# Head sums filled to the whole array, an offset joined to the bonus, and sums of squares in groups of four, in a kernel of an RWKV block, two expert layers and two attention blocks

## The chip, the cores and the metric

The kernel runs as one program on one core of a Trainium2 chip. The metric is the device time of one execution in microseconds (us), from a median of several runs. The core's engines are TensorE (PE; PEld is its loading of stationary operands), VectorE (DVE), ScalarE (ACT), GpSimd (POOL) and SyncE (SP, which here issues most DMA transfers). Each takes its own list of instructions in order, and the lists are held together by semaphores.

## What is computed

All arrays are float32; x has 512 rows of width 1024, a context has 256 rows. The program has two parts, one behind the other. The first has two layers of a token mixer and an expert layer of 16 experts: the mixer of layer 0 is a Fourier transform, that of layer 1 an RWKV recurrence in two directions. The second has two layers of four kinds of attention and an MLP. What the change touches of it:

```python
def rwkv_output(y, r, v, g, k_dirs, r_k, lnx_w, lnx_b, wo, dtype):
    mu = jnp.mean(y, axis=-1, keepdims=True)               # y: 512 x 16 heads x 64
    var = jnp.mean(jnp.square(y - mu), axis=-1, keepdims=True)
    yn = (y - mu) * lax.rsqrt(var + LNX_EPS)
    yn = yn.reshape(bsz, t, D_MODEL) * lnx_w + lnx_b
    bonus = sum(jnp.sum(r * k_d * rk, axis=-1, keepdims=True) for k_d in k_dirs) * v
    out = (yn + bonus.reshape(bsz, t, D_MODEL)) * g
    return out @ wo

def rms_norm(x, g):                                        # many of these
    return x * lax.rsqrt(jnp.mean(x * x, axis=-1, keepdims=True) + EPS) * g

h2 = rms_norm(x, norm2[l])                                 # second part, layer l
x = x + jnp.square(jax.nn.relu(h2 @ w_up[l])) @ w_down[l]
```

## The kernel before, in words

Activations lie transposed: the 1024 features are 8 blocks of 128 partitions (ND = 8), the tokens run along the free axis. A large product is written as three products of halves (`mm3`, lines L930 to L932): each operand is split by `split` (L894 on ACT, L895 on DVE or POOL) into a high and a low part, here `whi` and `wlo` for the weights that `wload` brings, block by block, through a DMA on SP into `wraw` (L914).

**The order.** The program is written down in Python with generators that take turns; a scheduler then orders each engine's list by its own estimates. Tiles come from pools with a fixed number of buffers, so a write into a buffer waits until its last reader is done.

**Sums of squares.** A norm over the 1024 features of a token needs a sum over partitions. Class `Sums` does it: `add` squares one block of features into a tile `sq` (L956 on POOL or DVE, L958 on ACT) and calls `flush`, which multiplies a block of ones (128 rows, 32 columns) by `sq` into the PSUM tile `nps` (L967). Block dt goes to the group of columns dt mod 4 of the array, so that four groups of 32 columns collect two blocks each. `flush` issues one product for each `sq` as soon as more than `lag` are outstanding. `col` copies the four groups (L976), adds them up (L979), and `rsqrt_col` and `bcast_col` take the root and spread it over partitions (L986 to L999). These sums stand in the norm ahead of the recurrence, in that ahead of the second expert layer (whose router products `lgT`, L801, also use a quarter of the columns each; its `psh`, L812, use the whole array), in the norm ahead of the MLP (`n2`, added to while `wo` is computed, with the products `up_` behind it) and in the norm of the next layer (added to while the MLP's second product `dn` is computed, one block of features after the other; each is 24 or more products of 128x512). How many `sq` may be outstanding follows from the number of buffers of the tag that `e.sq` names.

**The key projection** (`k_ahead`, `k_evac`, eight blocks m of 128 features). For block m, PE makes `cps` (running sums of the decay, L1275), ACT makes `Pe` and `Pi` of it (exponentials, L1276 and L1277, which need a table load on ACT), the projection `pj` gives `kt`, its norm per head goes over `kn`, `rn` (L1294 on ACT, L1295 on DVE) and `rnb` to `kk` (L1305). DVE and POOL make `kd`, `bkt` and `art` of them, which DMAs store. Last come `bon`, the head sums for the bonus (L1338, PE), `vm`, bonus times value (L1339, DVE), and the DMA that stores `vm` as `sp_bv` (L1340). The recurrence then loads `bk` and `ar` back (L1406, L1407; first used by `bkp`, L1439).

**The output of the recurrence** (`c_out`). Four token tiles of 128; `chain(t)` makes for each: `mu`, head means (L1671), `od`, the difference (L1672), its square `osq` on ACT (L1673), `var`, head sums of the squares with the table `hsum` as stationary operand (128 rows, 16 columns; eight products, L1677), `ors`, root and reciprocal on 16 partitions (L1679, L1680), `rsb`, the way back from 16 heads to 128 features with `hback` as stationary operand (16 rows, 128 columns, L1687), `gps`, the gate (128 rows, 128 columns, L1688). DVE multiplies `od` by weight and `rsb` (L1691), adds offset and bonus (L1692) and multiplies by the gate (L1694); ACT and DVE or POOL split the result into `oh` and `ol`. `project` multiplies by `rw_wo` (`wo`, 128x256 products) and adds to x (L1710). `weave` lets chains 1 and 2 go first, then chains 0 and 3 beside the products for tiles 1 and 2, then the products for tiles 0 and 3.

```python
hback = pa.tile([16, ND, P], F32, name="hback")
nc.sync.dma_start(hback, e.d["k_hback"].rearrange("p (a b) -> p a b", a=ND))
...
weave((chain(1), 12.0), (chain(2), 12.0))
weave((chain(0), 12.0), (chain(3), 12.0), (project(slice(1, 3)), 18.0))
weave((project(slice(0, 4, 3)), 1.0))
```

Of the kernel before, what the change touches and what calls it, by code (L numbers as in the profile page):

```python
# [11 lines left out]
F32 = mybir.dt.float32  # L12
F32R = mybir.dt.float32r
I32 = mybir.dt.int32
AF = mybir.ActivationFunctionType
ALU = mybir.AluOpType
# [3 lines left out]
P = 128  # L20
D = 1024
ND = 8
T = 512
# [16 lines left out]
def host_tables():  # L40
# [67 lines left out]
    a = np.zeros((P, 16))  # L108
# [14 lines left out]
    sel = np.zeros((P, ND, 16))  # L123
    for dt in range(ND):
        sel[:64, dt, 2 * dt] = 1.0
        sel[64:, dt, 2 * dt + 1] = 1.0
    add("hsum", sel.reshape(P, 128))
# [651 lines left out]
def route(e, l, pr, pq, pp, rt, NTt, hD, V, posm, before, after):  # L779
# [71 lines left out]
    e.sq = dict(tag="sq", bufs=4)  # L851
# [90 lines left out]
class Sums:  # L942


    def __init__(self, e, pool, pp, n, ndt=ND, tag="mm"):
        self.e, self.pool, self.pp, self.n, self.ndt, self.tag = e, pool, pp, n, ndt, tag
        self.ng = min(4, ndt)
        self.ps = pp.tile([P, 512], F32, name="nps0", tag=tag)
        self.due = []
# [12 lines left out]
    def flush(self, lag):  # L962
        e = self.e
        while len(self.due) > lag:
            dt, sq = self.due.pop(0)
            j = 32 * (dt % self.ng)
            e.nc.tensor.matmul(self.ps[j:j + 32, :self.n], e.t("ones")[:, 0:32], sq, start=dt < self.ng,  # L967
                               stop=dt + self.ng >= self.ndt, tile_position=(0, j))
# [117 lines left out]
def c_proj(e, sp, tg, PL, ch, h):  # L1086
    nc, tc = e.nc, e.tc
    tt_ = nc.vector.tensor_tensor
    with ExitStack() as ctx:
# [190 lines left out]
        def k_evac(m, pss):  # L1280
# [58 lines left out]
            tt_(vm, flat(ps, 4), vm, ALU.mult)  # L1339
            nc.sync.dma_start(sp["bv"][:, m, :], vm)  # L1340
# [289 lines left out]
def c_out(e, sp, tg, Y):  # L1630
# [4 lines left out]
    with ExitStack() as ctx:  # L1635
# [9 lines left out]
        hback = pa.tile([16, ND, P], F32, name="hback")  # L1645
        nc.sync.dma_start(hback, e.d["k_hback"].rearrange("p (a b) -> p a b", a=ND))
# [13 lines left out]
        hsum = e.tc_("hsum").rearrange("p (a b) -> p a b", a=ND)  # L1660
        nc.sync.dma_start(e.x, sp["x"])

        def chain(t):
# [12 lines left out]
            for dt in range(ND):  # L1676
                nc.tensor.matmul(ps[:16, :P], hsum[:, dt, :], sq[:, dt, :], start=dt == 0, stop=dt == 7)  # L1677
            rs = pw.tile([16, P], F32, name="ors")
            nc.scalar.activation(rs, ps[:16, :P], AF.Sqrt, bias=eps[:16], scale=1.0 / 64)  # L1679
            nc.vector.reciprocal(rs, rs)  # L1680
            yield 3.0
            for hf in range(2):
                ps = pm.tile([P, 4, P], F32, name="rsb", tag="mm")
                pg = pm.tile([P, 4, P], F32, name="gps", tag="mm")
                for b in range(4):
                    dt = hf * 4 + b
                    nc.tensor.matmul(ps[:, b, :], hback[:, dt, :], rs, start=True, stop=True)  # L1687
                    nc.tensor.matmul(pg[:, b, :], g2[:, dt * P:(dt + 1) * P], tg[:, ts], start=True, stop=True)  # L1688
                for b in range(4):
                    dt = hf * 4 + b  # L1690
                    nc.vector.scalar_tensor_tensor(d_[:, dt, :], d_[:, dt, :], e.pv["rw_lnx_w"][:, dt:dt + 1], ps[:, b, :], op0=ALU.mult, op1=ALU.mult)  # L1691
                    nc.vector.scalar_tensor_tensor(d_[:, dt, :], d_[:, dt, :], e.pv["rw_lnx_b"][:, dt:dt + 1], bv[:, dt, ts], op0=ALU.add, op1=ALU.add)  # L1692
                hs = slice(hf * 4, hf * 4 + 4)
                tt_(d_[:, hs, :], pg, d_[:, hs, :], ALU.mult)  # L1694
                split(e, d_[:, hs, :], oh[:, hs, ts], ol[:, hs, ts], nc.gpsimd if hf else nc.vector)
                yield 3.0
# [161 lines left out]
def stage_e(e, l, n1, more):  # L1858
# [4 lines left out]
    with ExitStack() as c1:  # L1863
# [6 lines left out]
        e.sq = dict(tag="u", bufs=3)  # L1870
# [3 lines left out]
        for fq in range(4):  # L1874
            up = (pw.tile([P, ND, T], F32R, name="uph"), pw.tile([P, ND, T], F32R, name="upl"))
            for f in range(8):
# [4 lines left out]
                u = pw.tile([P, T], F32, name="u", tag="u", bufs=3)  # L1881
# [25 lines left out]
def attention(e, l, c2, mixT, n1, pq, rsb2, w_up):  # L1907
# [316 lines left out]
    for _ in out_proj((4, 5), lambda m: n2.add(m, e.x[:, m, :], nc.gpsimd if m % 2 else None, lag=2)):  # L2224
        pass
# [124 lines left out]
```

## Time and profile before

| | |
|---|---|
| median of 3 runs | 3890.82 us (3889.8 to 3914.53) |
| profiled execution | 3894.26 us, of which the span is 3892.5 |
| mean granted clock of TensorE | 0.93 |
| busy: PE, DVE, ACT, POOL | 92%, 45%, 29%, 14% |
| sums of squares (L967) | 156 records, median 592 ns |
| key projection, from its first to its last block | about 1100 to 1285 us |
| output of the recurrence | about 1744 to 1839 us |
| MLP of the two attention layers, product dn | around 3084 to 3140 and 3836 to 3880 us |

All durations are of the one profiled execution. A float32 product that isn't split into halves by the program stands as two records in the trace, so the number of records is twice that of the products for `nps`, `var`, `rsb` and `gps`. A record's length covers the time until its last column has left the array; what a product costs in a stream is the distance from its start to the next start. The granted clock is a share of 2.4 GHz: 0.5 is the lower level, 1.2 GHz, and a window's number is the mean over both. Busy time of a group counts overlapping records once, its mean doesn't.

### The profile page before, as it was taken

To read this page: it belongs to the slowest core of one execution; us is meant where nothing else is said; L and a number is where in the kernel's file an instruction comes from. 1 tells how busy PE (TensorE), PEld (TensorE's weight loads), DVE (VectorE), ACT (ScalarE), POOL (GpSimd) and SP (SyncE) were. 2 spreads that over 40 slices of the span, in tenths; PEclk is the share of its full clock that TensorE was granted. 3 is DMA by queue.
4 is the path that set the end of the run, shared out by engine and by line. 5 is a ranking of instruction groups with operands and counts; after the bars stand their busy time and mean duration, and the time that the engine had idled before them with its cause. 6 is when DMAs were issued, how large, how long until landed. Compare 5 with 4: busy or idle time off the path is not lost. (4 is left out here: it accounts for less than half of the span.)

```text
span 3892.5 us, 66006 instructions
## 1 busy us (share of the span) xinstructions
PE 3585.0 (92%) x28088; PEld 2259.5 (58%) x28088; DVE 1762.6 (45%) x3424; ACT 1115.3 (29%) x1974; POOL 545.2 (14%) x429
## 2 busy tenths in 40 slices
PE   8889999978998686779999999999999989999999
PEld 4633333335777575668533324566788756567886
DVE  4512322246355566565221215865544458454443
ACT  3311111125366243332200002433322234342222
POOL 3100000002023122120100002220111222201111
PEclk8989999989998577788899999999999989999999
DMA  7489989934656644332899995111233321113332
GB/s 281 179 337 367 360 325 372 346 109 132 199 123 169 142 128 121 100 92 86 340 409 394 409 394 164 28 48 31 85 97 93 90 70 33 40 32 103 93 97 76
DMA packets 585853, 690.39 MB, mean 177 GB/s; under 512 B 178825, under 2 KB 454111, under 8 KB 585046
## 3 DMA queue, kind: packets, MB, share of 16 engines
q1 hardware_dynamic: 579344, 666.54, 50.6%
q10 hardware_dynamic: 3686, 11.09, 0.8%
q0 software_dynamic: 2528, 8.53, 0.6%
q8 instruction: 221, 3.62, 0.4%
q14 instruction: 74, 0.61, 0.0%
HBM read 646.24 MB, written 39.85 MB: 176 GB/s over the span
## 5 line engine op out<-in xcount | busy, mean ns | idle before, releaser
L894 ACT CAST whi<-wraw 128x1024 fp32r<-128x1024 f32 (+3 forms) x236 | 233.2, 989 | 707.2 <-issue 223.9
L641 PE MATMUL GU<-we,Xe 128*32 128x512 f32 x2048 | 304.4, 599 | 3.4 <-DVE hid L646 3.4
L895 DVE TENSOR_TENSOR wlo<-wraw,whi 128x1024 fp32r<-128x1024 f32 (+3 forms) x196 | 231.8, 1183 | 108.1 <-ACT whi L894 99.4
L666 PE MATMUL Y<-we,hidT 128*32 128x512 f32 x2048 | 261.3, 595 | 5.0 <-DVE Zc L698 3.5
L641 PE MATMUL GU<-we,Xq 128*32 128x512 f32 x2048 | 252.0, 611 | 0.0
L646 DVE TENSOR_TENSOR hid<-hid,GU 64x1536 f32<-64x1536 f32 (+1 forms) x32 | 47.7, 1491 | 359.4 <-ACT hid L645 359.4
L641 PE MATMUL GU<-we,Xc 128*32 128x512 f32 x1024 | 188.9, 596 | 0.0
L645 ACT ACTIVATE hid<-GU 64x1536 f32<-64x1536 f32 (+1 forms) x32 | 39.3, 1229 | 457.7 <-PE GU L641 457.7
L1884 POOL TENSOR_TENSOR u<-u 128x512 f32<-128x512 f32 x64 | 93.9, 1469 | 533.2 <-ACT uph L1883 533.2
L641 PEld LDWEIGHTS GU<-we,Xe 128*32 128x32 f32 x2048 | 78.8, 110 | 150.9 <-issue 145.2
L641 PEld LDWEIGHTS GU<-we,Xq 128*32 128x32 f32 x2048 | 67.7, 113 | 160.8 <-issue 157.9
L930 PE MATMUL pj<-hTh,whi 128*128 128x512 f32 (+1 forms) x352 | 154.5, 440 | 4.1 <-ACT hTh L1013 2.8
L666 PEld LDWEIGHTS Y<-we,hidT 128*32 128x32 f32 x2048 | 70.2, 110 | 148.1 <-issue 143.4
L932 PE MATMUL pj<-hTh,wlo 128*128 128x512 f32 (+1 forms) x352 | 148.7, 423 | 0.0
L931 PE MATMUL pj<-hTl,whi 128*128 128x512 f32 (+1 forms) x352 | 147.6, 419 | 0.0
L895 POOL TENSOR_TENSOR wlo<-wraw,whi 128x1024 fp32r<-128x1024 f32 x40 | 96.1, 2403 | 311.3 <-ACT whi L894 291.5
L930 PE MATMUL pj<-xh,whi 128*128 128x512 f32 (+1 forms) x320 | 118.2, 369 | 9.2 <-ACT whi L894 9.2
L1430 PE MATMUL Aps<-ar,bk 64*128 64x128 f32 (+1 forms) x768 | 98.3, 367 | 27.1 <-DVE GA L1434 25.1
L655 DVE COPY hidT<-htp 128x512 f32<-128x512 f32 (+1 forms) x48 | 27.6, 600 | 209.3 <-PE htp L654 121.4
L711 DVE SCALAR_TENSOR_TENSOR xres<-sps,mod,xres 128x512 f32<-128x512 f32 x128 | 89.0, 745 | 65.1 <-PE sps L710 64.5
L932 PE MATMUL pj<-xh,wlo 128*128 128x512 f32 (+1 forms) x320 | 115.4, 361 | 1.6 <-DVE wlo L895 1.6
L931 PE MATMUL pj<-xl,whi 128*128 128x512 f32 (+1 forms) x320 | 114.8, 359 | 0.0
(2151 smaller groups left out, 7929.4 us busy)
## 6 DMA issues: line engine op xcount, KB each, us to landing
we<-in_moe_wd_dram SPq DMA_DIRECT2D x128, 1024.0 KB
we<-in_moe_wg_dram SPq DMA_DIRECT2D x126, 1024.0 KB
we<-in_moe_wu_dram SPq DMA_DIRECT2D x126, 1024.0 KB
ada<-in_ada_w_dram SPq DMA_DIRECT2D x32, 1024.0 KB
wraw<-in_w_up_dram SPq DMA_DIRECT2D x64, 512.0 KB
wraw<-in_w_down_dram SPq DMA_DIRECT2D x64, 512.0 KB
wraw<-in_w_in_dram SPq DMA_DIRECT2D x42, 512.0 KB
adw<-in_ada_w_dram SPq DMA_DIRECT2D x32, 512.0 KB
```

The lines of the kernel that those rows point to most:

```text
L641: nc.tensor.matmul(GU[j:j + 32, g, :], xs[g][:, kk, :], ws[m][:, k, h * 512:(h + 1) * 512], start=kk == 0, stop=kk == 7, tile_position=(0, j))
L645: nc.scalar.activation(hid[up], GU[lo], AF.Silu)
L646: nc.vector.tensor_tensor(hid[up], hid[up], GU[up], ALU.mult)
L666: nc.tensor.matmul(Y[j:j + 32, 0, :], hidT[:, g, k, 32 * kh:32 * kh + 32], w[:, kh, h * 512:(h + 1) * 512], start=kh + k == 0, stop=kh * k ...
L711: nc.vector.scalar_tensor_tensor(r_[:, c, :], ps, g2[:, c, s:s + 1], r_[:, c, :], op0=ALU.mult, op1=ALU.add)
L894: e.nc.scalar.copy(hi, src)
L895: (eng or e.nc.vector).tensor_tensor(lo, src, hi, ALU.subtract)
L930: nc.tensor.matmul(ps, a[0], b[0], start=start, stop=False)
L931: nc.tensor.matmul(ps, a[0], b[1], start=False, stop=False)
L932: nc.tensor.matmul(ps, a[1], b[0], start=False, stop=stop)
L1430: nc.tensor.matmul(pss[hh][:, b, :64 * na], flat(4 * g + b)[hv[hh]], ar[hv[hh], 4 * g + b, 0:na, :], start=True, stop=True, tile_position= ...
L1884: nc.gpsimd.tensor_tensor(u, u, u, ALU.mult)
```

## The change

Three edits:

1. `flush` issues its products in steps: 4 where the tag of `sq` has more than four buffers, 2 where it has four, else 1, as soon as `lag` plus one step of them are outstanding. The tags get more buffers: six for `sq` behind the first expert layer's entry, and six for `u`, which the norm in the MLP uses. The norm ahead of the MLP has four buffers and its lag goes from 2 to 1.
2. In the key projection a new ACT operation adds the offset `rw_lnx_b` to `vm`, between DVE's product (L1339) and the DMA that stores it.
3. In `c_out`, `hback` becomes 128 rows with zeros in 112 of them (a memset on POOL ahead of the load), `hsum` is no longer a loaded table but is made on POOL (memset, then a copy) with 128 columns for each block, `ors` takes 128 partitions, and the 32 DVE operations that added offset and bonus become 8 that add the bonus alone, 512 columns each.

```diff
@@ class Sums
+        self.step = self.ng if e.sq["bufs"] > self.ng else min(2, self.ng) if e.sq["bufs"] > 3 else 1
@@ flush
-        while len(self.due) > lag:
-            dt, sq = self.due.pop(0)
-            j = 32 * (dt % self.ng)
-            e.nc.tensor.matmul(self.ps[j:j + 32, :self.n], e.t("ones")[:, 0:32], sq, start=dt < self.ng,
-                               stop=dt + self.ng >= self.ndt, tile_position=(0, j))
+        while len(self.due) >= lag + self.step:
+            for _ in range(self.step):
+                dt, sq = self.due.pop(0)
+                j = 32 * (dt % self.ng)
+                e.nc.tensor.matmul(self.ps[j:j + 32, :self.n], e.t("ones")[:, 0:32], sq, start=dt < self.ng,
+                                   stop=dt + self.ng >= self.ndt, tile_position=(0, j))
@@ buffers and lag
-    e.sq = dict(tag="sq", bufs=4)
+    e.sq = dict(tag="sq", bufs=6)
...
-        e.sq = dict(tag="u", bufs=3)
+        e.sq = dict(tag="u", bufs=6)
...
-                u = pw.tile([P, T], F32, name="u", tag="u", bufs=3)
+                u = pw.tile([P, T], F32, name="u", tag="u", bufs=6)
...
-    for _ in out_proj((4, 5), lambda m: n2.add(m, e.x[:, m, :], nc.gpsimd if m % 2 else None, lag=2)):
+    for _ in out_proj((4, 5), lambda m: n2.add(m, e.x[:, m, :], nc.gpsimd if m % 2 else None, lag=1)):
@@ k_evac
             tt_(vm, flat(ps, 4), vm, ALU.mult)
+            nc.scalar.activation(vm, vm, AF.Identity, bias=e.pv["rw_lnx_b"][:, m:m + 1])
             nc.sync.dma_start(sp["bv"][:, m, :], vm)
@@ c_out
-        hback = pa.tile([16, ND, P], F32, name="hback")
-        nc.sync.dma_start(hback, e.d["k_hback"].rearrange("p (a b) -> p a b", a=ND))
+        hback = pa.tile([P, ND, P], F32, name="hback")
+        nc.gpsimd.memset(hback, 0.0)
+        nc.sync.dma_start(hback[:16], e.d["k_hback"].rearrange("p (a b) -> p a b", a=ND))
+        hsum = pa.tile([P, ND * (P + 2)], F32, name="hsum")
+        nc.gpsimd.memset(hsum, 0.0)
+        nc.gpsimd.tensor_copy(hsum.rearrange("p (a b) -> p a b", a=ND)[:, :, 0:2], e.tc_("hsel").unsqueeze(1).to_broadcast([P, ND, 2]))
...
-        hsum = e.tc_("hsum").rearrange("p (a b) -> p a b", a=ND)
...
-                nc.tensor.matmul(ps[:16, :P], hsum[:, dt, :], sq[:, dt, :], start=dt == 0, stop=dt == 7)
-            rs = pw.tile([16, P], F32, name="ors")
-            nc.scalar.activation(rs, ps[:16, :P], AF.Sqrt, bias=eps[:16], scale=1.0 / 64)
+                nc.tensor.matmul(ps[:, :P], hsum[:, dt * P:(dt + 1) * P], sq[:, dt, :], start=dt == 0, stop=dt == 7)
+            rs = pw.tile([P, P], F32, name="ors")
+            nc.scalar.activation(rs, ps[:, :P], AF.Sqrt, bias=eps, scale=1.0 / 64)
...
-                    nc.vector.scalar_tensor_tensor(d_[:, dt, :], d_[:, dt, :], e.pv["rw_lnx_b"][:, dt:dt + 1], bv[:, dt, ts], op0=ALU.add, op1=ALU.add)
                 hs = slice(hf * 4, hf * 4 + 4)
+                tt_(d_[:, hs, :], d_[:, hs, :], bv[:, hs, ts], ALU.add)
```

How the lists of instructions change, at three places; a row is the line, the operation, what it writes and reads, its shape, and how many in a row. Lines of the changed kernel are up to five lower or three higher than before.

PE, in the product dn of layer 0's MLP (`dn` with two buffers' numbers, `uph` and `upl` its moving operand, `nps` the sum product, reading `sq` and the table of ones). Before, behind the first block of features:

```order
L931 MATMUL dn__24161<-upl,whi 128x512
L932 MATMUL dn__24161<-uph,wlo 128x512
L967 MATMUL nps_24118<-sq,tab 32x512
L930 MATMUL dn__24198<-uph,whi 128x512
L931 MATMUL dn__24198<-upl,whi 128x512
```

In the changed kernel, behind the fourth:

```order
L926 MATMUL dn__24257<-upl,whi 128x512
L927 MATMUL dn__24257<-uph,wlo 128x512
L965 MATMUL nps_24106<-sq,tab 32x512 x4
L925 MATMUL dn__24297<-uph,whi 128x512
L926 MATMUL dn__24297<-upl,whi 128x512
```

The sum products, one behind each of seven blocks and one at the end before, now stand in one row of four there and one at the end.

PE, in `c_out`, where the first two chains come to the head sums. Before:

```order
L1588 MATMUL Yps<-rc,SV 64x64 x16
L1677 MATMUL var<-osq,k_tabc 16x128 x16
L1687 MATMUL rsb<-ors,hback 128x128
L1688 MATMUL gps<-tg,g_15293 128x128
L1687 MATMUL rsb<-ors,hback 128x128
L1688 MATMUL gps<-tg,g_15293 128x128
```

In the changed kernel:

```order
L1587 MATMUL Yps<-rc,SV 64x64 x16
L1680 MATMUL var<-osq,hsum 128x128 x16
L1690 MATMUL rsb<-ors,hback 128x128
L1691 MATMUL gps<-tg,g_15301 128x128
L1690 MATMUL rsb<-ors,hback 128x128
L1691 MATMUL gps<-tg,g_15301 128x128
```

The order of the products stays; `var` writes 128 partitions in place of 16.

ACT, in the key projection's second block. Before:

```order
L1317 ACTIVATE kd<-a__7502,omka,pvt 128x768
L1269 ACTIVATE a__7503<-aps,pvt 128x512
L1269 ACTIVATE a__7503<-aps,pvt 128x256
L1317 ACTIVATE kd<-a__7503,omka,pvt 128x768
L1276 ACT_TABLE_LOAD
L1276 ACTIVATE Pe<-cps 128x512
```

In the changed kernel:

```order
L1315 ACTIVATE kd<-a__7503,omka,pvt 128x768
L1267 ACTIVATE a__7504<-aps,pvt 128x512
L1267 ACTIVATE a__7504<-aps,pvt 128x256
L1315 ACTIVATE kd<-a__7504,omka,pvt 128x768
L1338 ACTIVATE vm<-vm,pvt 128x512
L1274 ACT_TABLE_LOAD
L1274 ACTIVATE Pe<-cps 128x512
```

The new operation stands ahead of the table load for `Pe` and `Pi`, in six of the eight blocks; in the first it stands behind the first `Pe`, in the last at the end.

## Rows read from the trace of the kernel before

**Rows 1.** The page's part 1: busy us of each engine, share of the span, instructions.

```profile
PE 3585.0 (92%) x28088; PEld 2259.5 (58%) x28088; DVE 1762.6 (45%) x3424; ACT 1115.3 (29%) x1974; POOL 545.2 (14%) x429
```

**Rows 2.** Timeline of PE, layer 0's product dn: start, duration, line, out<-in, records.

```profile
3104.00 0.39 PE L931 MATMUL dn__24272<-upl,whi 128*128 128x512 f32 x1
3104.23 0.39 PE L932 MATMUL dn__24272<-uph,wlo 128*128 128x512 f32 x1
3104.55 1.04 PE L967 MATMUL nps<-sq,tab 128*32 128x512 f32 x2
3105.52 0.50 PE L930 MATMUL dn__24309<-uph,whi 128*128 128x512 f32 x1
```

**Rows 3.** Timeline of PE, the norm ahead of the second expert layer.

```profile
1839.20 1.08 PE L967 MATMUL nps<-sq,tab 128*32 128x512 f32 x8
...
1842.81 1.40 PE L812 MATMUL psh<-rt,mod 128*128 128x16 f32 x11
```

**Rows 4.** Windows: stretch, length, busy us (records) of PE, PEld, DVE, ACT, POOL; granted clock, DMA share, GB/s.

```profile
1748.50:1764.00 15.50, 15.50 (x66) 12.53 (x65) 13.54 (x32) 4.74 (x7) 0.00 (x0) 0.67 0.98 304
1786.00:1793.30 7.30, 7.30 (x33) 5.27 (x33) 2.50 (x10) 0.00 (x0) 0.00 (x0) 0.87 0.01 2
3084.00:3140.00 56.00, 55.00 (x219) 36.69 (x217) 22.67 (x20) 14.93 (x19) 13.58 (x9) 1.00 0.30 74
```

**Rows 5.** Timeline of PE in c_out, token tiles 1 and 2.

```profile
1755.41 0.80 PE L1688 MATMUL gps<-tg,g 128*128 128x128 f32 x2
1756.13 2.07 PE L1687 MATMUL rsb<-ors,hback 16*128 16x128 f32 x8
...
1762.14 2.08 PE L1688 MATMUL gps<-tg,g 128*128 128x128 f32 x8
```

**Rows 6.** Timeline of PE in c_out, token tile 0 and the output products after it.

```profile
1776.46 3.67 PE L1677 MATMUL var<-osq,k_tabc 128*16 128x128 f32 x32
...
1786.01 0.48 PE L1687 MATMUL rsb<-ors,hback 16*128 16x128 f32 x2
1786.42 0.49 PE L1688 MATMUL gps<-tg,g 128*128 128x128 f32 x2
...
1793.31 0.56 PE L930 MATMUL wo<-oh,whi 128*128 128x256 f32 x1
...
1798.33 0.28 PE L932 MATMUL wo<-oh,wlo 128*128 128x256 f32 x1
1798.44 0.28 PE L930 MATMUL wo<-oh,whi 128*128 128x256 f32 x1
```

**Rows 7.** DVE by line, 1747 to 1770 us: shapes, records, busy, mean ns, idle before.

```profile
L1692 DVE SCALAR_TENSOR_TENSOR od<-od,pvt,bvl 128x128 f32<-128x128 f32 x16 | 5.0, 344 | 0.0
L1691 DVE SCALAR_TENSOR_TENSOR od<-od,pvt,rsb 128x128 f32<-128x128 f32 x16 | 4.9, 340 | 2.0 <-PE rsb L1687 2.0
L1694 DVE TENSOR_TENSOR od<-gps,od 128x512 f32<-128x512 f32 x4 | 2.7, 681 | 0.0
```

**Rows 8.** Timeline of POOL, ahead of the recurrence: the nearest memset.

```profile
1268.74 0.31 POOL L1378 MEMSET M<- 128x256 f32 x1
```

**Rows 9.** Timeline of ACT, end of the key projection's seventh block.

```profile
1263.89 1.28 ACT L1276 ACT_TABLE_LOAD   x1
1265.18 0.60 ACT L1276 ACTIVATE Pe<-cps 128x512 f32<-128x512 f32 x1
...
1269.92 0.27 ACT L1294 ACTIVATE rn<-kn,tiny 128x12 f32<-128x12 f32 x1
```

**Rows 10.** Timeline of DVE, the same place.

```profile
1266.47 0.67 DVE L1339 TENSOR_TENSOR vm<-bon,vm 128x512 f32<-128x512 f32 x1
...
1271.94 0.22 DVE L1295 RECIPROCAL rn<-rn 128x12 f32<-128x12 f32 x1
```

**Rows 11.** Waits, 1100 to 1300 us: us in total, times, longest.

```profile
PE bkp L1439 <- DMA bk<-sp_bk: 23.2, 1, 23.2
...
PE cps L1275 <- DVE vm L1339: 12.2, 4, 3.1
```

More of the change, by code (lines that the diff above doesn't have):

```diff
@@ L122, in host_tables @@
     add("half16", a)
[L123 to L127, printed above, removed]
     sel = np.zeros((P, ND, P))
```

## The prediction

> **What bounds the kernel now.** I read the page's part 1 first: PE is busy for 92% of the span, DVE for 45% [rows 1], so work that is taken from PE's stream shortens the run wherever PE doesn't wait. Then I asked by window whether that holds in the stages that the change touches. In the product dn of the MLP PE is busy for 55.0 of 56 us at clock 1.00 with DMA at 0.30 [rows 4]: PE sets the time there. In c_out PE is never idle in 1748.5 to 1764 and 1786 to 1793.3, yet its granted clock is 0.67 and 0.87, so part of each stretch ran at the lower level, 1.2 GHz; DVE is busy for 13.5 of 15.5 us in the first and 2.5 of 7.3 in the second [rows 4]. So c_out has two different limits: PE with DVE close behind for token tiles 1 and 2, PE alone for tiles 0 and 3. The key projection is another case: PE waits there for DVE's vm (12.2 us in four waits, the longest 3.1), and when it ends PE stands still for 23.2 us until the stored rows come back by DMA [rows 11]. What an instruction costs there is read from waits, not from busy time.
>
> **Sums of squares.** A sum product nps that stands alone between products: 3104.23 to 3105.52 is 1.29 us from the dn product ahead of it to the one behind, against 0.23 between two dn products (3104.00 to 3104.23), so it costs 1.06 us [rows 2]. Four of them together (eight records, two to a product) take 1.08 us where one takes 1.04 [rows 2, 3]: a group of four costs what one did. By the order, layer 0's dn had seven alone and one at the end and has now two groups: 6 fewer stops. Layer 1 had eight and has groups of 4, 3 and 1: 5 fewer. The norm ahead of the MLP had eight in each layer and has 2, 1, 1, 2, 1, 1: 2 fewer in each, because the scheduler puts an output product between two halves of a pair. That makes 15 x 1.06 = 15.9 us off PE's stream. What is late next: the last sum of that norm now stands some 40 products further down, but six PSUM buffers take up_ products meanwhile, so I cost that at nothing (0 to +2 for both layers). In the norm ahead of the second expert layer the order also turns from single sums to fours, and I count nothing: rows 3 show its eight records side by side already, though the program alternates them with lgT. The norm ahead of the recurrence I hold at 0, give or take 1.
>
> **Head sums and their way back.** rsb uses 16 rows of the array, gps all 128. A product of either is two records. Where the two alternate at the full clock, a product takes 0.41 us, 0.21 per record (1786.01 to 1786.42) [rows 6]. At the lower clock it takes 0.72 (1755.41 to 1756.13), 0.36 per record, but eight records of one kind in a row take 2.07 and 2.08, 0.26 each with the last one's whole length in it [rows 5]. So 16 rows are no dearer by themselves; changing between the two is. Full-row products follow each other at the full clock in 0.11 (psh, eleven in 1.40, of which the last one's length is 0.28) [rows 3]. After the change all are full-row products: 0.11 per record. In the Trainium skill, "TensorEngine Tiling (Array Packing)", Key Properties, a change of tiling mode drains the TensorE; the alternating products agree with it, 0.21 against 0.11 per record.
>
> Tiles 1 and 2: PE's 64 records of this kind would need 64 x 0.112 = 7.2 us of the 15.5, 8.3 less. But DVE is the next limit: its 16 operations of L1692 (5.0 us busy) become four of 128x512 (0.68 each, 2.7), which is 2.3 less, and the 2.0 us for which it waits on rsb go [rows 7]. So 4.3 less, not 8.3. Tile 0: 7.3 us become 32 x 0.112 = 3.6, 3.7 less; DVE's 2.5 fit in it. Behind it 23 output products run from 1793.31 to 1798.33, 0.218 each, and the one after in 0.11 [rows 6]: the clock had fallen to the lower level during the alternation, and came back. I expect it not to fall when no product has 16 rows, for nothing else distinguishes these stretches from the full-clock ones on either side; at 0.115 the 23 take 2.6, 2.4 less. Tile 3 repeats the pattern from 1802.85, another 6.0. Sum: 4.3 + 6.1 + 6.0 = 16.4 less. If the clock falls all the same it is 4.8 to 7 fewer, so 9.5 to 11.5.
>
> Held at nothing: filling var from 16 columns to 128. Its 32 records take 3.67 us, 0.11 each [rows 6], the pace of psh with full columns [rows 3]; the dear end, each record at the alternating 0.21, would be 64 x 0.10 = +6.4. POOL's two memsets of some 1,024 columns: a 256-column one took 0.31 [rows 8], so 1.2 each. hback's load stands behind the first, and behind that load on SP stand those of bvl, of two rw_wo blocks and of the rest. I take 0, since DVE and PE have queued work then; but DMA is at 0.98 in this stretch [rows 4], so a late start can pass on whole: 0 to +2.5.
>
> **The offset joined to the bonus.** Eight ACT operations of 128x512 (about 0.6 each by Pe's row) are added, and each waits for DVE's vm; in blocks two to seven it stands right ahead of the table load for Pe and Pi, so all of them are behind it, and DVE's and POOL's work on those. In block seven ACT comes to the table load at 1263.89 [rows 9], while vm ends at 1266.47 + 0.67 = 1267.14 [rows 10]: ACT would stop 3.3 us, plus 0.6 for the operation. Worked the same way, the six blocks give stops from 0 to 3.4. If every microsecond passed on, that is about 14 + 4 = 18. But ACT and DVE have idle time later in each block, which I expect to leave about 0.25 a block over seven blocks, 1.8. In the last there is no later work to hide it: ACT's rn moves from 1269.92 to 1273.8 and ends at 1274.1, DVE's rn from 1271.94 to 1274.1 [rows 9, 10], 2.2 later, and the recurrence's first load behind it. Together +4, bounds 0 and 18.
>
> **Sum.** -15.9 - 16.4 + 4 = -28.3. The profiled execution took 3894.26 us (span 3892.5 and 1.8 around it), which gives 3866.0; it lies 3.4 above the median of 3890.82, so against the median the forecast is 3862.5. One per cent, about what a measurement of this kernel can tell from no change, is 38.9.
>
> **Rivals.**
> (1) The weight load, not the change between modes, sets the pace of the alternating products: then full rows cost as much as 16, and c_out gains only DVE's 2.3. -15.9 - 2.3 + 4 = -14.2, 3876.6. For it: loads and products overlap, and rows 5 are at the lower clock alone. Against it: psh loads full weights at 0.11. The Trainium skill, "TensorE: Matmul & The Clock Gate", LDWEIGHTS, has the load's time go by columns and not by the contraction's rows; by that rule alone filling rsb's rows brings nothing.
> (2) Everything on PE passes on in c_out (8.3 + 6.1 + 6.1 = 20.5) and vm's stops vanish in idle time: -36.4, 3854.4. DVE's 13.5 of 15.5 us [rows 4] speaks against the first half.
> (3) Slower: ACT's stop closes a ring. Pe late makes cps late (its PSUM buffers are given back by Pe, Pi and vm), PE already waits up to 3.1 there [rows 11], and the next vm comes later by as much. Price: 3.3 + 0.6 + 3.1 = 7.0 in each of seven blocks, +49; with the 32.3 gained elsewhere +16.7, 3907.5. It decides from 32.3 / 7 = 4.6 a block. Against it: ACT waits for PE in each block anyway.
> (4) The change doesn't do what it says: the four sums run one after the other, so nothing is saved: 3878.4. Rows 3 speak against it.
>
> **How the numbers follow.** Forecast 0.58 (its own range 3855 to 3872), (1) 0.16, (2) 0.15, (3) 0.07, (4) 0.04. The range 3845 to 3882 leaves out (3), part of (4), and the fast end of (2). Faster by over 1%, below 3851.9: half of (2) and a sixth of the forecast, 0.17. Slower by over 1% would take (3) at more than its price: 0.03. Within: 0.80.
>
> **What would show it.** Right: dn's stretch 6 shorter with two nps groups of eight records; rsb and gps at 0.11 per record in c_out, at clock 1.00; wo without a slow stretch; DVE busy throughout tiles 1 and 2; ACT idle up to 3.4 ahead of vm, the recurrence's first load about 4 later. Wrong: rsb still at 0.2 (rival 1), a clock below 1 in 1786 to 1798 with full rows, or blocks of the key projection longer by over a microsecond each (rival 3).

## The result, and the profile after it

The changed kernel takes 3847.37 us, the median of 4 runs (3841.41 to 3855.55), against 3895.66 us before (4 runs; the 3 that the forecast had gave 3890.82): ratio 0.987, 95% interval 0.983 to 0.991. Two further comparisons gave 0.988 (0.986 to 0.990) and 0.989 (0.988 to 0.991). So it is faster by 1.0 to 1.3%, 39 to 49 us between medians; the forecast was 28 us, less than one per cent. Its profiled execution took 3855.55 us (span 3853.8).

The page's part 1, as [rows 1]:

```profile
PE 3551.1 (92%) x28088; PEld 2247.6 (58%) x28088; DVE 1760.6 (46%) x3400; ACT 1120.9 (29%) x1982; POOL 546.4 (14%) x432
```

PE's share of the span is the same as before; the busy times of PE and of the span fell together.

In the product dn of layer 0, to be held against [rows 2], four sums stand in one group:

```profile
3084.14 0.40 PE L927 MATMUL dn__24257<-uph,wlo 128*128 128x512 f32 x1
3084.47 1.06 PE L965 MATMUL nps<-sq,tab 128*32 128x512 f32 x8
3085.46 0.50 PE L925 MATMUL dn__24297<-uph,whi 128*128 128x512 f32 x1
```

The group, eight records, costs 1.32 us from the dn product ahead to the one behind, less the 0.23 that two dn products stand apart: 1.09, where one alone cost 1.06.

PE in c_out, as [rows 5] (tiles 1 and 2, first fence) and [rows 6] (tiles 0 and 3, second), then the windows there, as [rows 4]:

```profile
1751.66 0.39 PE L1690 MATMUL rsb<-ors,hback 128*128 128x128 f32 x2
...
1752.35 1.13 PE L1690 MATMUL rsb<-ors,hback 128*128 128x128 f32 x8
1758.04 1.67 PE L1691 MATMUL gps<-tg,g 128*128 128x128 f32 x8 [4.56 <-DVE od L1694]
```

```profile
1780.73 0.38 PE L1690 MATMUL rsb<-ors,hback 128*128 128x128 f32 x2
1780.95 0.39 PE L1691 MATMUL gps<-tg,g 128*128 128x128 f32 x2
...
1784.22 0.36 PE L925 MATMUL wo<-oh,whi 128*128 128x256 f32 x1
...
1791.43 0.38 PE L1690 MATMUL rsb<-ors,hback 128*128 128x128 f32 x2
```

```profile
1760.00:1780.00 20.00, 20.00 (x142) 17.53 (x143) 15.01 (x24) 8.71 (x13) 4.72 (x3) 0.95 0.30 83
1780.00:1800.00 20.00, 19.44 (x169) 19.23 (x167) 13.57 (x31) 2.48 (x4) 1.29 (x1) 1.00 0.01 2
1800.00:1825.00 25.00, 24.38 (x208) 22.30 (x212) 7.88 (x17) 5.09 (x8) 1.28 (x1) 1.00 0.07 19
```

A product of two records, rsb or gps, now takes 0.22 us where it took 0.41, and from tile 0's first record, at 1780.73, to the output product behind the last, at 1784.22, it is 3.5 us in place of 7.3. The granted clock is 1.00 in both later windows. In tiles 1 and 2 PE now waits 4.6 us for DVE, and there alone the clock drops, behind that wait (0.95 in the first window). The waits of that stretch (1746 to 1770 us) show what holds DVE's list, a cast of weights that ACT could not begin before its load had landed:

```profile
ACT whi L889 <- DMA wraw<-in_rw_wo_dram: 7.5, 2, 5.7
...
PE gps L1691 <- DVE od L1694: 4.6, 1, 4.6
...
DVE wlo L890 <- ACT whi L889: 2.3, 1, 2.3
```

ACT and DVE at the end of the key projection, as [rows 9, 10]; the number in brackets is the idle time ahead of the row and what ended it:

```profile
1254.92 0.72 ACT L1338 ACTIVATE vm<-vm,pvt 128x512 f32<-128x512 f32 x1 [3.32 <-DVE vm L1337]
...
1261.44 0.27 ACT L1292 ACTIVATE rn<-kn,tiny 128x12 f32<-128x12 f32 x1
```

```profile
1254.21 0.68 DVE L1337 TENSOR_TENSOR vm<-bon,vm 128x512 f32<-128x512 f32 x1
...
1261.74 0.23 DVE L1293 RECIPROCAL rn<-rn 128x12 f32<-128x12 f32 x1 [0.57 <-ACT rn L1292]
```

ACT stops 3.32 us ahead of vm, then spends 0.72 on it. The forecast had 3.3 and 0.6.

Where did the other 20 us come from? I lined up the traces on PE, product by product (the n-th of each kind), and took the differences of the start times. The table gives, for each stage, by how much it is longer or shorter than in a second trace of the kernel before (the run before_again below; the first one is in the table too); the other columns are runs that the next section explains. "Sums of squares" stands for the two norms ahead of the MLP and the two dn products.

| us | before, first trace | changed | after_again | after_base | sums_only | tab_only | after_tab | hback128 |
|---|---|---|---|---|---|---|---|---|
| up to the norm ahead of the recurrence, with it (to 866) | -0.6 | +1.9 | +0.9 | 0.0 | +3.9 | +8.0 | +1.8 | +0.1 |
| projections of r and v (to 1105) | +0.7 | -14.2 | -14.5 | -10.6 | +2.8 | -13.1 | -1.2 | +2.9 |
| key projection, to the recurrence's first product | -0.5 | +2.0 | +2.3 | +1.1 | -0.9 | +2.5 | +5.2 | +0.4 |
| recurrence (to 1740) | -7.1 | +0.6 | +0.9 | -7.8 | -0.6 | +0.3 | +3.0 | -0.3 |
| c_out | 0.0 | -14.8 | -14.9 | -13.2 | +0.5 | -0.7 | -15.4 | -11.9 |
| second expert layer | +0.1 | -2.1 | -2.3 | -1.4 | -3.0 | -2.7 | -1.5 | -1.4 |
| attention, both layers | +1.6 | -1.4 | -1.4 | -1.4 | -1.2 | 0.0 | -1.4 | +2.9 |
| sums of squares | 0.0 | -16.7 | -16.7 | -16.6 | -16.7 | 0.0 | -16.7 | 0.0 |
| end | -5.8 | -44.7 | -45.7 | -49.9 | -15.2 | -5.7 | -26.2 | -7.3 |

Two things stand out. The sums of squares gained what was forecast within 1 us, and c_out within 2 (within 3.2 in after_base). And the projections of r and v, which no term of the forecast names, gained another 11 to 15. The first trace of before, on which the forecast rested, was itself some 6 us shorter than the second.

In the projections (waits from 900 us to their end; us in total, times, longest), before and after, each with its window:

```profile
DVE wlo L895 <- ACT whi L894: 58.1, 13, 7.5
...
ACT whi L894 <- DMA wraw<-in_rw_wr_dram: 15.8, 4, 7.5
...
PE pj L930 <- ACT whi L894: 9.2, 9, 1.6
```

```profile
900.00:1100.00 200.00, 185.40 (x1117) 141.21 (x1117) 78.79 (x109) 93.05 (x156) 22.93 (x14) 0.98 0.59 172
```

```profile
DVE wlo L890 <- ACT whi L889: 37.2, 11, 8.3
...
ACT whi L889 <- DMA wraw<-in_rw_wr_dram: 2.1, 5, 0.9
...
PE pj L925 <- ACT xh L889: 0.4, 1, 0.4
```

```profile
900.00:1087.00 187.00, 185.47 (x1117) 138.54 (x1116) 79.84 (x111) 93.97 (x157) 22.36 (x14) 0.99 0.62 184
```

PE has the same work, 185.4 and 185.5 us of it. Before, it was idle for 14.6 of 200 us; after, for 1.5 of 187. It no longer waits for weights (9.2 us before), and ACT's cast hardly waits for their load any more (15.8 us became 2.1 for r). No line of this stage was edited. But the edit of c_out took hsum, 128 columns, out of a table that is loaded ahead of the recurrence, and with a shorter load the scheduler put the lists of this stage in another order; the next section tests this. SP before and after, from one block of r to the next (start, time to issue, what is loaded or stored; adw are weights of the modulation, wraw those of r, sp_r is the store of a finished block):

```profile
948.04 0.37 SPq L914 DMA_DIRECT2D wraw<-in_rw_wr_dram  x1
953.99 0.37 SPq L1117 DMA_DIRECT2D adw<-in_ada_w_dram  x1
956.06 0.34 SPq L1204 DMA_DIRECT2D sp_r<-rm  x1
956.49 0.39 SPq L1117 DMA_DIRECT2D adw<-in_ada_w_dram  x1
956.97 0.53 SPq L914 DMA_DIRECT2D wraw<-in_rw_wr_dram  x1
```

```profile
937.41 0.37 SPq L909 DMA_DIRECT2D wraw<-in_rw_wr_dram  x1
937.87 0.55 SPq L1115 DMA_DIRECT2D adw<-in_ada_w_dram  x1
941.34 0.34 SPq L1202 DMA_DIRECT2D sp_r<-rm  x1
943.17 0.37 SPq L1115 DMA_DIRECT2D adw<-in_ada_w_dram  x1
944.56 0.37 SPq L909 DMA_DIRECT2D wraw<-in_rw_wr_dram  x1
```

Before, a block takes 8.9 us (wraw to wraw), after it 7.2. The cycle of four is the same, but the new list begins with one more block of weights ahead of the first store, and on PE the modulation's products stand in fours between those of r in place of eights.

### The profile page after: what moved, and what is told of

Same layout as the page of the kernel before. It is cut to its first block, busy times and chain, and to the rows that moved or that the text cites. A ratio compares the mean times of both kernels' runs of the same rounds, so it can differ in the third digit from the quotient of the medians.

```text
span 3853.8 us, 65974 instructions
## 1 busy us (share of the span) xinstructions
PE 3551.1 (92%) x28088; PEld 2247.6 (58%) x28088; DVE 1760.6 (46%) x3400; ACT 1120.9 (29%) x1982; POOL 546.4 (14%) x432
```

## Experiments

Was the gain in the projections the order's, or a difference between executions? Four kernels on one chip.

after_again is the changed kernel once more.

> The changed kernel once more, for a second trace of it. Its first trace, lined up with that of before product by product on PE, is 38.7 us ahead at the end: 13.8 of these come in the projections of r and v (900 to 1100 us), 15.9 in c_out, 16.6 at the sums of squares; it loses 2.4 at the end of the key projection and some 8 in the recurrence (1300 to 1650 us), and wins 7.5 in the second attention layer, where no instruction moved. Theory: the 13.8 belong to the changed kernel and stand here again, within 2 us; the 8 and the 7.5 are differences between executions and come out otherwise. Rival: the 13.8 too are a difference between executions, and here that stretch is within 3 us of before. Ratio about 0.987 in either case.

Measured: 0.988 (0.986 to 0.990), and the projections 14.5 us shorter (table). The 8 us in the recurrence stand against the first trace of before again, but not against the second. So the gain in the projections repeats.

after_tab is the changed kernel with the table left in:

```diff
     add("half16", a)
+    sel = np.zeros((P, ND, 16))
+    for dt in range(ND):
+        sel[:64, dt, 2 * dt] = 1.0
+        sel[64:, dt, 2 * dt + 1] = 1.0
+    add("hsum", sel.reshape(P, 128))
```

> The changed kernel, with the table hsum still in the constants that are loaded ahead of the recurrence (512 bytes per partition, not read). With it the lists of all engines in the projections of r and v are those of before again. Theory, order: the shorter load changes the scheduler's estimate, and with it the order of the modulation products, of weights' loads on SP and of casts there, and this is where 13.8 us came from; so this kernel is 12 to 14 us slower than the changed one, ratio to before about 0.990, and its projections take as long as before's within 3 us. Rival: the order is worth nothing and the stretch differs between executions; then ratio 0.987 as for the changed kernel.

Measured: 0.993 (0.991 to 0.996), 3873.81 us against 3853.12 of after_again on the same chip, so 21 us slower, where 12 to 14 were expected. In the trace the projections are 1.2 us shorter than before, not 14; PE's products stand there in the order of before, and so does SP's whole list. The theory of the order holds; the other falls. The rest of the 21 us stands in the trace mostly in the key projection and the recurrence, where traces of one kernel differ as much.

tab_only makes the opposite test, before without the table:

```diff
-    add("hsum", sel.reshape(P, 128))
...
+        hsum = pa.tile([P, ND * 18], F32, name="hsum")
+        nc.gpsimd.memset(hsum, 0.0)
+        nc.gpsimd.tensor_copy(hsum.rearrange("p (a b) -> p a b", a=ND)[:, :, 0:2], e.tc_("hsel").unsqueeze(1).to_broadcast([P, ND, 2]))
```

> Before, with the table hsum taken out of the loaded constants and made on POOL in c_out, still 16 columns for each block; nothing else. Theory, order: -12 to -14 us, ratio about 0.9967, all of it between 900 and 1100 us. Rival, difference between executions: ratio 1.000.

Measured: 0.995 (0.994 to 0.997), 18 us between medians, and -13.1 us in the projections, where PE and SP have the order of the changed kernel. Its trace as a whole ends only 5.7 us ahead, above all because it is 8.0 longer ahead of this stage; that execution was the slowest of the eight. By the medians, an edit that takes 512 bytes per partition out of a load is worth about as much as the sums of squares (22 us) or the filled rows (13 us) below.

sums_only is before with the first edit alone.

> Before, with the grouped sums of squares alone. Forecast: -15.9 us, ratio 0.9959; on PE 6.4 in layer 0's dn, 5.3 in layer 1's, 2.1 in each norm ahead of the MLP, nothing in the norm ahead of the second expert layer. Rival: groups gain nothing, ratio 1.000.

Measured: 0.994 (0.992 to 0.996). In the trace -7.1 in layer 0's dn, -5.9 in layer 1's, -1.8 and -1.9 in the norms: 16.7, forecast 15.9.

The next four asked for a second trace of before, whether the shorter load itself is the gain, and what in c_out is.

> The kernel before once more, for a second trace of it. All four traces taken since show the recurrence (1300 to 1740 us) 7 to 10 us longer than the first trace of before, and the second attention layer 6 to 8 shorter, also where nothing there was changed. Theory: the first trace of before is the odd one, and this one is like the four in both places. Rival: something in the kernels since changes both; then this trace is like the first, within 2 us.

Measured: 3900.07 us. It is 7.1 us longer than the first trace in the recurrence and 6 us shorter in the second attention layer, as the others are. So this trace came out as expected, but the theory that the first one was the odd one does not hold: later traces are as short in the recurrence, of before with small edits (pad64 -6.4, hback64 -6.5) as of the changed kernel (after_base -7.8). It is something that comes and goes between executions.

pad64 is tab_only with 64 columns of zeros in the table's place:

```diff
+    add("hpad", np.zeros((P, 64), np.float32))
```

> As the kernel before with hsum made on POOL, but 64 columns of zeros are loaded in place of the table's 128, so the load is half as much shorter. The list of SP is that of before, row for row, and PE's differs in 12 rows. Theory, order: with the order of before the gain is gone; ratio 1.000 within 0.2%, and 900 to 1100 us take as long as in before, within 3 us. Rival, the shorter load itself gives the time: half of tab_only's gain, some 7 us of it between 900 and 1100 us, ratio 0.998.

Measured: 1.000 (0.998 to 1.001), projections 2.5 us shorter than the second trace of before and 3.2 than the first. The order of the products on PE and of the transfers on SP is that of before throughout. With half of the shorter load and before's order the gain is gone, so it is the order and not the shorter load that gives it.

hback128 fills rsb alone:

```diff
-        hback = pa.tile([16, ND, P], F32, name="hback")
+        hback = pa.tile([128, ND, P], F32, name="hback")
+        nc.gpsimd.memset(hback, 0.0)
...
-            rs = pw.tile([16, P], F32, name="ors")
+            rs = rss[t % 2]
```

> Before, with rsb's stationary operand filled from 16 to 128 rows (zeros) and its moving operand too; var, the table and the 32 DVE operations stay. Theory, change of mode: rsb and gps follow each other in 0.11 us per record where they alternate, the clock stays at 1.00 in c_out, and c_out takes about 12 to 15 us less, ratio 0.9965. Rival, weight load: 0.21 per record as before; c_out within 3 us of before, ratio 1.000.

hback64 is the same with 64 rows.

> As hback128, but filled to 64 rows only, half of the array. Theory, change of mode: 64 rows are still another mode than gps's 128, so alternating records keep 0.21 us and nothing is gained but perhaps the clock. Rival, the number of idle rows is what costs: about half of hback128's gain, 0.16 per record.

Measured: hback128 0.997 (0.995 to 0.998), c_out 11.9 us shorter; hback64 one run of 3893.3 us, c_out 5.6 shorter. hback64 gained the half of hback128, but not as its rival had it: the price per record stayed, as the theory said, and it is the clock, which the theory had left open, that gave the half. Products of hback128, then of hback64, which alternate on PE, and the windows of the output products in hback64 and in the second trace of before:

```profile
1760.20 0.39 PE L1691 MATMUL rsb<-ors,hback 128*128 128x128 f32 x2
1760.43 0.39 PE L1692 MATMUL gps<-tg,g 128*128 128x128 f32 x2
```

```profile
1758.66 0.49 PE L1691 MATMUL rsb<-ors,hback 64*128 64x128 f32 x2
1759.07 0.49 PE L1692 MATMUL gps<-tg,g 128*128 128x128 f32 x2
1759.49 0.48 PE L1691 MATMUL rsb<-ors,hback 64*128 64x128 f32 x2
```

```profile
1790.00:1820.00 30.00, 29.39 (x197) 25.26 (x196) 15.77 (x44) 2.48 (x4) 2.72 (x2) 1.00 0.00 1
```

```profile
1760.00:1775.00 15.00, 15.00 (x51) 11.04 (x51) 12.60 (x35) 5.84 (x7) 1.06 (x1) 0.54 0.75 249
1795.00:1825.00 30.00, 30.00 (x161) 26.20 (x161) 15.51 (x43) 2.40 (x4) 1.45 (x1) 0.77 0.00 1
```

At 64 rows a product still takes 0.42 us, as with 16, and with 128 it takes 0.22: what costs is that the two differ, not how many rows are idle. It agrees with the Trainium skill, "TensorEngine Tiling (Array Packing)", Key Properties, by which a change of tiling mode drains the TensorE. That products of 16 or 64 rows run in another mode than those of 128 is my reading; no run shows it by itself. But with 64 rows the clock stays at 1.00 in 1790 to 1820, where before's is 0.77 in the like stretch. Since the pace at the full clock is the same, the 5.6 us are the clock's share (by one run of hback64), and the rest of the 11.9 is what the alternation cost. 3 us more, up to the changed kernel's 14.8, come with DVE's shorter list and the other edits there; no run takes these apart.

Then the offset. novm leaves the ACT operation out, so the offset is missing from its output; poolvm has it done by POOL:

```diff
-            nc.scalar.activation(vm, vm, AF.Identity, bias=e.pv["rw_lnx_b"][:, m:m + 1])
+            nc.gpsimd.tensor_scalar(vm, vm, e.pv["rw_lnx_b"][:, m:m + 1], None, op0=ALU.add)
```

> The changed kernel without the ACT operation on vm, so its output leaves out the offset of the normalisation. Against the second trace of before the changed kernel loses some 2 us between the projections' end and the recurrence's start. Theory: these 2 (2.0 to 2.6) are the price of ACT's stop ahead of vm, and nearly all of it stands in the last block; without it PE reaches the recurrence's first product 2 to 3 us earlier. Rival, as forecast: stops in each block cost 4 together, 6 where the order of the projections is before's; then the blocks before the last are shorter too. Second rival: 0, the new order of the projections costs it.

> The changed kernel with the offset added to vm by POOL in place of ACT. Theory: ACT no longer stops, and POOL has time after its bkt, so the 2 us come back as without the operation. Rival: POOL stops at vm in ACT's place and its part of bkt and a_ comes late; then key projection and tail are as in the changed kernel or up to 4 us longer.

Measured, single runs: novm 3865.31 us, key projection +2.2; poolvm 3849.49 us, key projection -3.0. So by the whole stage the operation costs nothing: +2.2 without it against +2.0, +2.3 and +1.1 with it. But the blocks ahead of the last differ by more than that between traces whatever the kernel: from the second block's first cps to the eighth's they take 145.8 and 146.6 us in before's two traces, 145.8 to 151.4 with the operation on ACT and 143.2 to 151.2 in all other kernels. The last block doesn't spread. Its first cps and the last rnb products, in before, in the changed kernel and in novm:

```profile
1261.46 2.64 PE L1275 MATMUL cps<-k_tabc,sg 128*128 128x128 f32 x20
...
1272.30 2.83 PE L1303 MATMUL rnb<-tab,rn 128*64 128x128 f32 x24 [3.15 <-DVE rn L1295]
```

```profile
1249.20 2.64 PE L1273 MATMUL cps<-k_tabc,sg 128*128 128x128 f32 x20
...
1262.12 2.83 PE L1301 MATMUL rnb<-tab,rn 128*64 128x128 f32 x24 [1.30 <-DVE rn L1293]
```

```profile
1254.11 2.64 PE L1273 MATMUL cps<-k_tabc,sg 128*128 128x128 f32 x20
...
1264.88 2.83 PE L1301 MATMUL rnb<-tab,rn 128*64 128x128 f32 x24 [3.08 <-DVE rn L1293]
```

From one to the other it is 10.8 us before, 12.9 in the changed kernel and 10.8 in novm. All six traces with the operation on ACT have 12.9 (after, after_again, after_base, after_tab, n2four, n2four_b), all eleven without it 10.7 to 10.9, the two with it on POOL 11.1. So the operation costs 2.1 us in the last block, and 0.3 when POOL does it.

n2four was to hold the sums of the norm ahead of the MLP until four are there.

> The changed kernel with the sums of squares of the norm ahead of the MLP held until four are there (lag 0): by the order two pairs and a four in each layer in place of six stops, so 3 stops where the changed kernel has 6. Forecast from 1.06 us a stop: 3.2 less in each layer, 6.4 together. Rival: four buffers are too few, squares wait for their buffers and PE for squares; then 0, or slower.

The kernel that ran under this label did not have that edit; it gives the program's very last norm six buffers in place of four, and PE's order is that of the changed kernel. A single run took 3851.67 us, and it serves as one more trace of the changed kernel: end -48.6, projections -10.9. The edit ran later, as n2four_b and within best:

```diff
+    n2.sums.step = 4
-    for _ in out_proj((4, 5), lambda m: n2.add(m, e.x[:, m, :], nc.gpsimd if m % 2 else None, lag=1)):
+    for _ in out_proj((4, 5), lambda m: n2.add(m, e.x[:, m, :], nc.gpsimd if m % 2 else None, lag=0)):
```

> The changed kernel on the chip of the next three, as their measure. Ratio to before 0.988; its trace against the second one of before: 44 to 46 us ahead at the end.

> The changed kernel with the sums of squares of the norm ahead of the MLP held until four are there (lag 0) and nothing else: by the order 2, 2 and 4 in each layer, three stops where the changed kernel has six. Forecast from 1.06 us a stop: 3.2 less in each layer. Rival: four buffers are too few, squares wait for buffers and PE for squares; then 0 or slower.

> The changed kernel with the offset added to vm by POOL and the sums of the norm ahead of the MLP held until four are there (stops of 2, 2 and 4 in each layer, three in place of six). Its parts: POOL's version was 5 us ahead of the changed kernel at the end of the key projection (a single trace), three stops fewer in each layer are 6.4 us at 1.06 each. Theory: both add, 8 to 11 us faster than the changed kernel, ratio to before 0.985. Rival: the key projection's gain is given back while the recurrence waits for its loads, and squares wait for buffers; then as the changed kernel, 0.988.

Measured on one chip: after_base 0.989 (0.988 to 0.991), best 0.986 (0.984 to 0.987), 13 us less; n2four_b, a single run, 3853.36 us. after_base's trace ends 49.9 us ahead, where 44 to 46 were expected: it is the one that is short in the recurrence. In n2four_b each norm is 2.8 to 2.9 us shorter than before, against 1.8 to 1.9 in the changed kernel: 1 us gained per layer, not 3.2. PE's waits for squares around the first of them:

```profile
PE nps L965 <- ACT sq L955: 0.7, 1, 0.7
PE nps L965 <- POOL sq L953: 0.5, 1, 0.5
```

The last sums stand right behind their squares now, and PE waits 1.2 us for these: part of the stops came back as waits. best has the lowest ratio of the study, but its trace is only 2.4 us ahead of after_base's at the end, and its key projection is 4.5 us longer than before, though its last block is 1.9 shorter than after_base's. The traces show about 4 us of the 13, 2 in the norms and 2 in that block; the rest stays open.

Last, what in the new order is the gain? r_act takes the store of r off SP, adw_pool the modulation's loads, adw_pool_r both:

```diff
-                nc.sync.dma_start(sp["r"][:, m, :], rm)
+                nc.scalar.dma_start(sp["r"][:, m, :], rm)
...
-                    nc.sync.dma_start(ws[i], e.d["ada_w"][1, h * T:h * T + T, n * 256:n * 256 + 256].rearrange("(k p) n -> p k n", p=P))
+                    nc.gpsimd.dma_start(ws[i], e.d["ada_w"][1, h * T:h * T + T, n * 256:n * 256 + 256].rearrange("(k p) n -> p k n", p=P))
```

> Before, with one edit: the store of the projection r (sp_r) is issued by ACT in place of SP. In before's list on SP the load of the weights two blocks on stands behind this store, which waits for the block's product; in the changed kernel it stands ahead of it. With the store off SP nothing but the loads for the modulation stands ahead of the weights. Theory: this place behind the store is what cost 8 to 9 us per block of r in place of 7.5; so the stretch of r (930 to 985 us) gets 5 to 9 us shorter, ratio 0.998. Rival: the eight modulation products in a row, or the loads for them, are what cost the time; then the stretch is within 2 us of before.

> Before, with one edit: the loads for the modulation (adw) are issued by POOL in place of SP. The scheduler then orders the modulation's products on PE in fours between pj products in place of eights, as in the changed kernel, while on SP the weights of r still stand behind the store of the block before last. Taking that store alone off SP gained nothing that can be measured. Theory now: the modulation (its loads ahead of the weights on SP, its products in eights at the end of a block) is what cost the time; the stretch of r gets 8 to 10 us shorter and r and v together 12 to 15, ratio to before 0.9965. Rival: it takes both, the store and the modulation, so this alone gives less than half.

> As adw_pool, and the store of r is issued by ACT: nothing stands ahead of the weights on SP any more. Theory, modulation: as adw_pool within 2 us. Rival, both are needed: 12 to 15 us less than before here, and under 7 in adw_pool.

Measured: 1.001 (0.999 to 1.003), 1.000 (0.998 to 1.003) and 1.000 (0.998 to 1.002). From the first product of r to the first of v, lined up with the second trace of before, the changed kernel gains 11.1 us (10.1 and 7.6 in after_again and after_base), tab_only 11.1, r_act 3.3, adw_pool 9.7 and adw_pool_r 9.6; traces with before's order lie from 2.4 longer to 1.5 shorter. So my theory of the store fell. In this stretch it is moving the modulation, its loads off SP and its products in fours, that brings most of the gain. The window of adw_pool:

```profile
925.00:990.00 65.00, 61.71 (x351) 41.02 (x350) 29.71 (x40) 31.63 (x53) 18.21 (x19) 0.95 0.72 225
```

PE is busy for 61.7 of 65 us there. But over the first two blocks of v adw_pool and adw_pool_r lose 7 us again, the changed kernel 1.4, and no ratio moved. Whether the loads' place or the products' makes the gain in r, and why the new order keeps it in v, stays open: that the order of the lists is the cause is shown, what in it is not.

## Why the prediction was wrong

**The step that failed is the list of what the change removes.** "Held at nothing" named var's filling and POOL's two memsets. That hsum is no longer a loaded table is told with the change itself, and the sum has no term for it. I looked at the order only where the edits' own operations stand. Had I compared the lists of SP and PE through the whole program, the other order in the projections would have been seen, together with the row that it bears on: PE idle for 14.6 of 200 us there, ACT's casts waiting for weights. It is worth 11 to 15 us in the traces, and 18 to 21 between medians (tab_only, after_tab). The forecast's own terms came near: 16.7 and 14.8 gained, 2.0 lost, 29.5 against 28.3. That the measured time still lies within 3845 to 3882 is luck: the range reached that far for rival (2), and the gain came from a stage that no rival names.

**The base.** The forecast's sum was made against a trace that was 6 us shorter than the second of the same kernel. The changed kernel's trace ends 38.9 us ahead of the first and 44.7 ahead of the second; either is well beyond the 28.3 forecast.

**Sums of squares: right.** 15 stops at 1.06 gave 15.9; measured 16.7 (16.6 in one trace). The rows of one group beside those of a single sum carried it. Rival (4) is out.

**c_out: right, in size and place.** Tiles 1 and 2: 4.3 forecast. The first rsb of tile 0 stood at 1786.01 and stands at 1780.73; the recurrence's end was 2.2 ahead, so 3.1 were won. Tile 0: 6.1 forecast; the first rsb of tile 3 went from 1802.85 to 1791.43, 11.4 ahead, so 6.1 were won. From there to the end of c_out another 5.4 to 5.6, forecast 6.0. var's filling cost nothing, as held: from its first product to rsb's first it is 3.6 us before and after (5.3 in after_base alone, whose c_out gained 1.6 less). The clock stayed up in tiles 0 and 3, as expected; in tiles 1 and 2 it still fell, behind PE's wait. DVE became the limit in tiles 1 and 2, as said, though not busy throughout. Behind it stands the weights' load: the cast that waited 5.7 us begins 25.2 us after c_out's first product, 23.6 before: 1.6 later, within the 0 to +2.5 held for that load. Rival (2) is out there.

Rival (1) fell with hback128: 0.22 a product in place of 0.41. By the Trainium skill, "TensorE: Matmul & The Clock Gate", LDWEIGHTS, a load's time goes by its columns and not by the rows of the contraction. The traces agree: a load of rsb's weights takes 0.18 us (median) with 16 rows and 0.19 with 128. But the pace of the alternating products changed all the same, so the load is not what sets it here.

**vm: right in the last block, not seen in the others.** ACT stops 3.3 us as worked out, and rn comes late by just that: ACT's at 1261.44 is 8.5 us ahead of before's, where the stage before it was 12.3 ahead, so 3.8 late against 3.9 forecast; DVE's at 1261.74 is 2.1 late against 2.2. The last block is 2.1 us longer in every trace with the operation. The other 1.8, a quarter of a microsecond in each block, can't be told from the spread of the blocks ahead. Forecast +4, seen +1.1 to +2.3 in the new order. In that, the second half of rival (2), stops that vanish in idle time, came true for the blocks ahead. Rival (3), the ring, is out: it decides from 4.6 us a block, and the six blocks ahead together take 145.8 to 146.4 us in three traces of the changed kernel, against 145.8 and 146.6 before.

**The norm ahead of the recurrence** was held at 0, give or take 1. The table's first row takes in all that lies ahead of it and differs by up to 8.0 where nothing was edited. The norm itself, from the expert layer's last product to the modulation's first, is 1.3 us longer in each trace of the changed kernel, so a little more than held.

## What to carry to other kernels

Where a scheduler writes the lists, the cost of an edit is also that of the order it changes elsewhere: compare the whole lists of every engine, SP's first, and look up what PE waits for in each stage that moved. Where products with different numbers of rows of the array alternate, try to fill the smaller with zeros: here it halved the time of each, the products themselves cost no more for it, and it kept the clock up as well. Take two traces before a sum is made against one: two of the same kernel differed by up to 8 us within one stage. And read the price of a small edit where traces agree (the last block here, within 0.1 us), not from a stage that spreads by more.

## What had not been expected of the hardware

In hback64, half-filled rows kept the clock and did not bring the pace: with 64 rows the products alternate at 0.42 us each as with 16, at granted clock 1.00 where 16 rows have 0.77. PE is busy for 29.4 of 30 us in the one window and for all 30 in the other. The expectation had left the clock open. What in the 16-row products brought it down, no run shows.
